# Gated DeltaNet's chunk inverses by products of nilpotent powers, and two buffers for the Mamba decays' tiles

## The chip, the cores and the metric

The kernel runs on one core of one Trainium2 chip. The metric is device time in microseconds (us), the median of three runs. Engines are named as in the profile: PE is TensorE (PEld its weight loads), DVE is VectorE, ACT is ScalarE, POOL is GpSimd, SP is SyncE, which issues the DMAs.

## The reference, cut to what matters

The model is a two-layer diffusion backbone in f32. Each layer runs three bidirectional mixers side by side on one input projection: S5, gated DeltaNet (GDN) and Mamba-2 (m2). One output projection takes all three; then comes a feed-forward part, dense SwiGLU in layer 0 and a mixture of experts in layer 1. There are 256 context and 256 latent tokens. The change is in GDN, which per chunk of tokens solves a unit lower triangular system:

```python
decay = seg_decay(gc)
lower = jnp.where(strict, jnp.einsum("bhnid,bhnjd->bhnij", kb, k) * decay, 0.0)
sol = lax.linalg.triangular_solve(jnp.eye(CHUNK) + lower, rhs,
                                  left_side=True, lower=True, unit_diagonal=True)
u_c, w_c = sol[..., :dv], sol[..., dv:]
def step(s, inp):
    v_new = u_i - w_i @ s
    s_next = s * gl_i + kd_i.T @ v_new
    o = qd_i @ s + a_i @ v_new
```

Four heads of width 128 and two directions (the second runs the tokens backwards) go through this. The kernel forms the inverse of `I + lower` itself, on blocks of 128 tokens instead of 64, and applies it by matmuls. For Mamba-2, the matrices `exp(cs_i - cs_j)` of 16 heads are the "decays".

## The kernel before, in words

The 512 tokens are four blocks t = 0..3 of 128; 0 and 1 are context, 2 and 3 latent. GDN needs one inverse X per block t, direction d and head. `inverses(gr)` (L919) makes them for two (t, d) at a time, four heads each, so every tile is 128 x 512. Four groups, grs[0] to grs[3], make the eight (t, d) of a layer; the two layers make 16.

Every group starts from an X that holds the inverses of the 16 x 16 diagonal blocks (POOL, L924). Three doublings follow, for blocks of 16, 32 and 64 (`LEVELS`). One doubling is: four transposes of X on PE (L933); four ACT evictions, one a head, that scale by beta (iv_Z, L936); four matmuls kw·Z (`mm4`, whose matmuls all have the helper's line L162); a DVE eviction that multiplies by the level's mask (iv_Q, L940); four matmuls W·X; a DVE eviction that subtracts from X (iv_X, L943). So a (t, d) makes nine trips from PE to an evicting engine and back, each needing the one before it. The matmuls of one `mm4` go to one PSUM bank, which `ps()` takes in turn from three banks ("px") in the order of the program; GDN's PE groups therefore run in program order, at most three banks apart.

The program order is: grs[0], grs[1], `steps(0)`, grs[2], `steps(1)`, in layer 0 `outs((0, 1))`, grs[3], `steps(2)`, `steps(3)`, `outs((2, 3))`. A `step` carries the state: r = v − k·S on DVE (gd_r, L963), X·r on PE, the state's update (gd_vk, gd_S), then the output A·vb (gd_vb, gd_A, gd_o). `outs` squares the outputs on ACT (gd_jk, L1013), scales them on POOL (gd_o, L1018), transposes them on PE (L1024), gates them (gd_y) and writes them to DRAM (yD).

`m2_decays` (L1060) makes the decays of four heads and one block at a time: two POOL selects, PE sums, an Exp on ACT (dq_W, L781), and a DMA to DRAM (WD, L1067). dq_W has four buffers. It makes 16 such tiles in layer 0 and 8 in layer 1. Mamba-2's later steps read them back; its tiles are m_in, m_S, m_E, m_yo, m_z and m_sq, and its last step is a norm (m_sq) and a write to yD. The output projection (tiles yr, yo; matmuls "yo,wH" and "yo,wL") reads yD back; in layer 0 in two parts, the first from S5's and GDN's rows, the second from Mamba's.

Nothing of the order around this is written out by hand. A scheduler places all instructions before the run, by the priority bands (`self.band`) that stand in Q0 and Q1, and by its own estimate of durations. Each engine then runs its list strictly in order.

Of the kernel before, what the change touches and what calls it, by code (L numbers as in the profile page):

```python
# [10 lines left out]
F32 = mybir.dt.float32  # L11
# [3 lines left out]
OP = mybir.AluOpType  # L15
# [12 lines left out]
U0, QKV0, ZG0, ZM0, XBC0 = 0, 512, 2048, 2576, 3600  # L28

CST = ["ident", "ones", "le", "ge", "gt", "lt", "blk16"]  # L30
LEVELS = [16, 32, 64]

Q0 = dict(
    pb=1.0, sc=2.5, tl=1.5, th=0.5, nb=7.5, db=1.9, ab1=0.85, ab2=3.0, sb=3.5, u=1.02, st=0.6, qkv=1.0, g0=2.0,
# [19 lines left out]
def _cst():  # L54
    i = np.arange(128)
    r, c = i[:, None], i[None, :]
    out = [r == c, np.ones((128, 128)), r <= c, r >= c, r > c, r < c, r // 16 == c // 16]
    for b in LEVELS:
        mf = ((r // b) % 2 == 1) & (c // b == r // b - 1)
        out += [mf, mf.T]  # L60
    c16 = np.arange(16)[None, :]
    out += [c16 == r % 16, c16 > r % 16, c16 < r % 16, (r // 16) % 2 == np.arange(2)[None, :]]
    return np.concatenate([np.asarray(m, np.float32) for m in out], axis=1)
# [27 lines left out]
class Net:  # L91
    def __init__(self, ctx, tc, A, out, dump=None):
        self.tc, self.nc, self.A, self.out, self.dump = tc, tc.nc, A, out, dump or {}
        nc = self.nc
        self.cpool = ctx.enter_context(tc.tile_pool(name="const", bufs=1))
        self.wstack = ctx.enter_context(ExitStack())
        self.wpool = self.wstack.enter_context(tc.tile_pool(name="wts", bufs=2, side="right"))
        self.dram = ctx.enter_context(tc.tile_pool(name="scr", bufs=1, space=DRAM))
        self.psum = ctx.enter_context(tc.tile_pool(name="psum", bufs=1, space=PSUM))
        self.psum_split(mm=(0, 1), px=(2, 3), bg=(4, 5, 6, 7), ad=(6, 7))  # L100
        c = self.cpool
        ncst = len(CST) + 2 * len(LEVELS)
        cst = c.tile([128, ncst * 128 + NC16], F32, name="cst")
        self.bands, self.ma, self.cur = {}, {}, None
        nm = len(CST) * 128
        nc.sync.dma_start(cst[:, 0:nm], A["cst"][:, 0:nm])
        with self.band(1.7):
            nc.sync.dma_start(cst[:, nm:], A["cst"][:, nm:])

        def mat(j):  # L110
            return cst[:, j * 128:(j + 1) * 128]

        for j, n in enumerate(CST):
            setattr(self, n, mat(j))
        self.mt = {}
        for j, b in enumerate(LEVELS):
            self.mt[b, 0] = mat(len(CST) + 2 * j)
            self.mt[b, 1] = mat(len(CST) + 2 * j + 1)
        c16 = cst[:, ncst * 128:]
        self.id16, self.up16, self.lo16, self.half16 = c16[:, 0:16], c16[:, 16:32], c16[:, 32:48], c16[:, 48:50]  # L120
        self.tri_r = c.tile([128, 2, 128], F32R, name="tri_r")
        nc.vector.tensor_copy(self.tri_r[:, 0, :], self.gt)
        nc.vector.tensor_copy(self.tri_r[:, 1, :], self.lt)
        self.pp = [c.tile([128, NPP], F32, name=f"pp{l}") for l in range(2)]
        for l in range(2):
            with self.band(0 if l == 0 else 1.7):
                nc.sync.dma_start(self.pp[l], A["pp"][l])
        self.epst = c.tile([128, 1], F32, name="epst")
        nc.vector.memset(self.epst, EPS)
        self.mods = [c.tile([128, 48, 2], F32, name=f"mods{l}") for l in range(2)]  # L130
        self.xT = c.tile([128, KT, T], F32, name="xT")
# [763 lines left out]
    def gdn(self, l, p, kT, qT, vD, kD, prep, nrm, bs, ks, qss, sm, szD, yD, t0, b0):  # L895
# [7 lines left out]
        def v4(ps):  # L903
            return ps.rearrange("p (h c) -> p h c", h=4)
# [13 lines left out]

        def inverses(gr):  # L919

            X = {}
            for t, d in gr:
                X[t, d] = p.tile(sh, F32, name="iv_X", bufs=Q[l]["iv"])
                nc.gpsimd.tensor_tensor(X[t, d].rearrange("p h (b c) -> p h b c", c=16),  # L924
                                        x16[d][:, 4 * t:4 * t + 4].unsqueeze(2).to_broadcast([128, 4, 8, 16]),
                                        self.blk16.rearrange("p (b c) -> p b c", c=16).unsqueeze(1).to_broadcast([128, 4, 8, 16]),
                                        op=OP.mult)
            for b in LEVELS:
                Z, W = {}, {}
                for t, d in gr:  # L930
                    pz = self.ps()
                    for h in range(4):
                        nc.tensor.transpose(pz[:, h * 128:(h + 1) * 128], X[t, d][:, h], self.ident)  # L933
                    Z[t, d] = p.tile(sh, F32, name="iv_Z", tag="iv_Z", bufs=2)
                    for h in range(4):
                        nc.scalar.activation(Z[t, d][:, h], pz[:, h * 128:(h + 1) * 128], AF.Copy, scale=bs[:, t, d, h:h + 1])  # L936
                for t, d in gr:
                    pq = mm4(lambda h: kw[t][:, h], lambda h: Z[t, d][:, h])
                    W[t, d] = p.tile(sh, F32, name="iv_Q", tag="iv_Q", bufs=2)
                    nc.vector.tensor_tensor(W[t, d], v4(pq), self.mt[b, d].unsqueeze(1).to_broadcast(sh), op=OP.mult)  # L940
                for t, d in gr:
                    px = mm4(lambda h: W[t, d][:, h], lambda h: X[t, d][:, h])
                    nc.vector.tensor_tensor(X[t, d], X[t, d], v4(px), op=OP.subtract)  # L943
            return X

        def load(t):
# [6 lines left out]
        def step(t, d, Y, last):  # L953
# [17 lines left out]
                    nc.scalar.activation(qs[:, h], pqs[:, h * 128:(h + 1) * 128], AF.Copy, scale=cs[:, h:h + 1])  # L971
            pw = mm4(lambda h: Y[:, h], lambda h: r[:, h])
            if not last:
                vk = p.tile(sh, F32, name="gd_vk", tag="iv_Q", bufs=2)
                nc.vector.tensor_tensor(vk, v4(pw), col(ks[:, t, d, :]), op=OP.mult)
                pu = mm4(lambda h: ktk[t][:, h], lambda h: vk[:, h])
                if old is not None:
                    nc.gpsimd.tensor_tensor(old, old, col(sm["tot"][:, d, t, 16:20]), op=OP.mult)
                    nc.vector.tensor_tensor(old, v4(pu), old, op=OP.add)
                else:  # L980
                    S[d] = p.tile(sh, F32, name=f"gd_S{d}", bufs=1)
                    nc.scalar.activation(S[d], v4(pu), AF.Copy)
# [24 lines left out]
        def outs(pair):  # L1007
# [12 lines left out]
            for h in (0, 2):  # L1020
                po = self.ps()
                for i in range(2):
                    for j, t in enumerate(pair):
                        nc.tensor.transpose(po[:, (2 * i + j) * 128:(2 * i + j + 1) * 128], os[t][:, h + i], self.ident)  # L1024
                y = p.tile([128, 2, 256], F32, name="gd_y", tag="iv_Z", bufs=2)
                nc.sync.dma_start(y, szD[:, h:h + 2, c])
                nc.vector.scalar_tensor_tensor(y, po.rearrange("p (h c) -> p h c", h=2), self.prm(l, "gng"), y, op0=OP.mult,
                                               op1=OP.mult)
# [31 lines left out]
    def m2_decays(self, p, sm, WD, first):  # L1060

        nc = self.nc
        for h0 in (0, 4, 8, 12):
            for t in range(first, 4):
                W = p.tile([128, 4, 128], F32, name="dq_W", bufs=4)
                self.decay_quad(p, sm, t, h0, W, "bg", 2)
                nc.sync.dma_start(WD[:, t, h0:h0 + 4], W)  # L1067

# [927 lines left out]
```

## Time and profile before

| | us |
|---|---|
| median of three runs (2482.48 to 2491.93) | 2483.15 |
| the profiled execution's own time | 2479.87 |
| its span in the trace | 2478.1 |
| PE busy in it | 2296.1 |
| DVE busy | 1868.1 |
| ACT busy | 1419.7 |
| POOL busy | 257.3 |

The profile is one execution, 3.28 us below the median. Its span leaves 1.8 us of its own time outside. The busy times overlap, so they don't add to the span. PE is busy for 93% of it, but that is an average: GDN's stretches are at 280 to 600 us (layer 0) and 1385 to 1590 us (layer 1), and there PE waits; from 1640 us on the layer-1 experts stream their weights and GDN has no part in it. A PE record's duration contains the time to pass through the array, so records in a row overlap; what a matmul costs is read from the distance of starts or from a stretch with its count.

### The profile page before, as it was taken

What the parts mean: (1) busy time and instruction counts of PE and PEld (TensorE: products, weight loads), DVE (VectorE), ACT (ScalarE), POOL (GpSimd) and SP (SyncE); (2) the same over time, 40 slices, a digit from 0 to 9 for tenths busy, and PEclk for the clock granted to TensorE, in tenths of its full rate; (3) what the DMA queues carried; (4) which work ended last, traced back from release to release, by engine and by line L of the source; (5) the groups of instructions that cost most, each with busy time, mean ns of one, the idle gap of its engine ahead of it and who ended that gap; (6) DMA issues with size and microseconds to landing.
All of it is one profiled execution on the core that took longest, in us unless ns stands there. A gap on an engine that the chain in (4) does not pass through costs nothing.

```text
span 2478.1 us, 36217 instructions
## 1 busy us (share of the span) xinstructions
PE 2296.1 (93%) x12886; PEld 1843.6 (74%) x12886; DVE 1868.1 (75%) x3138; ACT 1419.7 (57%) x2200; POOL 257.3 (10%) x332
## 2 busy tenths in 40 slices
PE   7999887898999999998998799889999999999998
PEld 4878675666767777886887677778887888888876
DVE  8887995576577773436679867678888888888887
ACT  4765475343335343235764844357777777677765
POOL 0011553212000000000021522100000000000000
PEclk9999998997999999998999899989999999999999
DMA  7443336994455755323444474478999999999994
GB/s 254 134 125 121 112 122 215 268 277 146 122 204 176 255 179 185 94 89 101 149 135 130 157 209 123 133 290 316 332 335 362 349 338 337 356 342 341 354 344 167
DMA packets 222378, 543.86 MB, mean 219 GB/s; under 512 B 25584, under 2 KB 105456, under 8 KB 186096
## 3 DMA queue, kind: packets, MB, share of 16 engines
q1 hardware_dynamic: 222192, 541.49, 63.7%
q8 instruction: 103, 1.69, 0.3%
q14 instruction: 83, 0.68, 0.1%
HBM read 487.87 MB, written 53.54 MB: 218 GB/s over the span
## 4 chain that ended last, share of the span: by engine, by line
PE 65%; DVE 6%; DMA 5%; ACT 4%; issue 3%; POOL 0%; SPq 0%; ACTq 0%; DVEq 0%; POOLq 0%
PE bank L162 62%; DMA ada<-in_ada_w_dram 1%; ACT mwH L1673 1%; DVE mwL L1674 1%; DVE wL L322 1%; PE bank L1761 1%; DMA wr<-in_w_in_dram 1%; DVE s5B L612 0%; DMA s5X<-XD 0%; DVE s5t L609 0%; DVE cv_acc L800 0%; DMA vD<-gd_tok 0%; PE bank L933 0%; DMA s5V<-VD 0%; DMA yr<-yD 0%
## 5 line engine op out<-in xcount | busy, mean ns | idle before, releaser
L1674 DVE TENSOR_TENSOR mwL<-mwr,mwH 128x2048 fp32r<-128x2048 f32 (+1 forms) x272 | 605.1, 2226 | 96.5 <-PE bank L162 60.3
L1673 ACT ACTIVATE mwH<-mwr 128x2048 fp32r<-128x2048 f32 (+1 forms) x272 | 508.2, 1869 | 201.6 <-PE bank L162 168.8
L321 ACT ACTIVATE wH<-wr 128x512 fp32r<-128x512 f32 (+2 forms) x388 | 232.8, 605 | 389.6 <-PE bank L162 241.2
L322 DVE TENSOR_TENSOR wL<-wr,wH 128x512 fp32r<-128x512 f32 (+2 forms) x388 | 267.0, 690 | 209.5 <-ACT wH L321 204.7
L162 PE MATMUL bank<-mwL,xeH 128*128 128x512 f32 (+1 forms) x768 | 292.7, 381 | 9.3 <-DVE mwL L1674 9.3
L162 PE MATMUL bank<-mwH,xeL 128*128 128x512 f32 (+1 forms) x768 | 288.1, 375 | 0.0
L162 PE MATMUL bank<-mwH,xeH 128*128 128x512 f32 (+1 forms) x768 | 284.7, 376 | 2.5 <-ACT mwH L1673 2.5
L162 PE MATMUL bank<-hH,wH 128*128 128x512 f32 (+2 forms) x656 | 245.8, 383 | 32.0 <-ACT cv_acc L798 18.6
L162 PE MATMUL bank<-hH,wL 128*128 128x512 f32 (+2 forms) x656 | 245.6, 376 | 8.7 <-DVE wL L322 8.5
L162 PE MATMUL bank<-hL,wH 128*128 128x512 f32 (+2 forms) x656 | 246.6, 376 | 1.1 <-DVE hL L300 1.1
L162 PEld LDWEIGHTS bank<-mwL,xeH 128*128 128x128 f32 x768 | 144.3, 188 | 37.7 <-DVE mwL L1674 11.7
L162 PEld LDWEIGHTS bank<-hH,wH 128*128 128x128 f32 (+1 forms) x656 | 124.0, 190 | 61.7 <-ACT cv_acc L798 20.7
L162 PEld LDWEIGHTS bank<-mwH,xeH 128*128 128x128 f32 x768 | 144.1, 188 | 32.3 <-ACT mwH L1673 3.3
L162 PEld LDWEIGHTS bank<-mwH,xeL 128*128 128x128 f32 x768 | 144.3, 188 | 26.3
L800 DVE SCALAR_TENSOR_TENSOR cv_acc<-cv_raw,pp,cv_acc 128x512 f32<-128x512 f32 (+1 forms) x192 | 152.8, 811 | 7.5 <-ACT cv_acc L796 5.8
L162 PEld LDWEIGHTS bank<-hH,wL 128*128 128x128 f32 (+1 forms) x656 | 124.4, 190 | 33.7 <-DVE wL L322 10.7
L162 PE MATMUL bank<-yo,wH 128*128 128x512 f32 (+1 forms) x512 | 133.2, 351 | 11.5 <-ACT yo L1387 7.7
L162 PEld LDWEIGHTS bank<-hL,wH 128*128 128x128 f32 (+1 forms) x656 | 124.7, 190 | 25.3 <-DVE hL L300 2.9
L162 PE MATMUL bank<-fhH,wH 128*128 128x512 f32 x352 | 137.6, 394 | 2.7 <-ACT fhH L299 1.8
L162 PE MATMUL bank<-mwL,eaH 128*128 128x512 f32 x352 | 139.2, 395 | 0.0
L162 PE MATMUL bank<-mwH,eaL 128*128 128x512 f32 x352 | 138.6, 394 | 0.0
L162 PE MATMUL bank<-fhL,wH 128*128 128x512 f32 x352 | 137.9, 392 | 0.0
(449 smaller groups left out, 4531.2 us busy)
## 6 DMA issues: line engine op xcount, KB each, us to landing
mwr<-in_moe_gu_dram SPq DMA_DIRECT2D x176, 1024.0 KB, 5.7
mwr<-in_moe_dn_dram SPq DMA_DIRECT2D x80, 1024.0 KB, 6.0
wr<-in_w_in_dram SPq DMA_DIRECT2D x160, 256.0 KB, 2.9
ada<-in_ada_w_dram SPq DMA_DIRECT2D x24, 1024.0 KB, 7.1
wr<-in_w_out_dram SPq DMA_DIRECT2D x64, 256.0 KB, 2.7
ada<-in_ada_w_dram SPq DMA_DIRECT2D x32, 512.0 KB, 6.0
wr<-in_ffn_w_gate_dram SPq DMA_DIRECT2D x44, 256.0 KB, 2.7
wr<-in_ffn_w_up_dram SPq DMA_DIRECT2D x44, 256.0 KB, 2.8
```

Source lines behind the costliest of these rows:

```text
L162: return self.nc.tensor.matmul(*a, **k)
L321: nc.scalar.activation(wH, w, AF.Copy)
L322: nc.vector.tensor_tensor(wL, w, wH.bitcast(F32), op=OP.subtract)
L800: nc.vector.scalar_tensor_tensor(acc, raw[:, :, j:j + 256], w[:, j:j + 1], acc, op0=OP.mult, op1=OP.add)
L1673: nc.scalar.activation(wH, w, AF.Copy)
L1674: nc.vector.tensor_tensor(wL, w, wH.bitcast(F32), op=OP.subtract)
L1761: nc.tensor.transpose(pt[:, j * 128:(j + 1) * 128], a[:, j * 128:(j + 1) * 128], self.ident)
```

## The change

The new `inverses` transposes X0 once and then uses a closed form. With X0 the block diagonal part's inverse and G the strictly block-triangular remainder in X0's frame, eight blocks of 16 make G⁸ = 0, so the inverse is (I − G)(I + G²)(I + G⁴)X0, read from the right side as the code builds it. F is G's mirror image, needed because PE wants the left factor transposed: G² = mm(F, G). Per (t, d): four transposes and four ACT evictions (before: twelve and twelve); masks on DVE for G and F; G² evicted by ACT (iv_G2); X −= G·X and X += G²·X on DVE; T = G²·X evicted by ACT (iv_T); X += G²·T on DVE. That is eight PSUM banks a (t, d) instead of nine, and six dependent trips from PE to an evicting engine and back instead of nine.

In numbers over both layers: PE transposes 192 → 64, PE matmuls of 128 x 128 in the inverses 384 → 448; DVE evictions of 128 x 512 96 → 80; ACT evictions of 128 x 128 192 → 64, and 32 new ones of 128 x 512. The six level masks become two masks. iv_Z and iv_Q (with the tiles that share their tags: gd_y, gd_vk) have three buffers instead of two, dq_W two instead of four. All priorities stay.

```diff
-LEVELS = [16, 32, 64]
-    for b in LEVELS:
-        mf = ((r // b) % 2 == 1) & (c // b == r // b - 1)
-        out += [mf, mf.T]
+    out += [c // 16 > r // 16, c // 16 < r // 16]
...
-            for b in LEVELS:
-                Z, W = {}, {}
-                for t, d in gr:
-                    pz = self.ps()
-                    for h in range(4):
-                        nc.tensor.transpose(pz[:, h * 128:(h + 1) * 128], X[t, d][:, h], self.ident)
-                    Z[t, d] = p.tile(sh, F32, name="iv_Z", tag="iv_Z", bufs=2)
-                    for h in range(4):
-                        nc.scalar.activation(Z[t, d][:, h], pz[:, h * 128:(h + 1) * 128], AF.Copy, scale=bs[:, t, d, h:h + 1])
-                for t, d in gr:
-                    pq = mm4(lambda h: kw[t][:, h], lambda h: Z[t, d][:, h])
-                    W[t, d] = p.tile(sh, F32, name="iv_Q", tag="iv_Q", bufs=2)
-                    nc.vector.tensor_tensor(W[t, d], v4(pq), self.mt[b, d].unsqueeze(1).to_broadcast(sh), op=OP.mult)
-                for t, d in gr:
-                    px = mm4(lambda h: W[t, d][:, h], lambda h: X[t, d][:, h])
-                    nc.vector.tensor_tensor(X[t, d], X[t, d], v4(px), op=OP.subtract)
+            for t, d in gr:
+                pz = self.ps()
+                for h in range(4):
+                    nc.tensor.transpose(pz[:, h * 128:(h + 1) * 128], X[t, d][:, h], self.ident)
+                Z[t, d] = p.tile(sh, F32, name="iv_Z", tag="iv_Z", bufs=3)
+                for h in range(4):
+                    nc.scalar.activation(Z[t, d][:, h], pz[:, h * 128:(h + 1) * 128], AF.Copy, scale=bs[:, t, d, h:h + 1])
+            for t, d in gr:
+                pg = mm4(lambda h: kw[t][:, h], lambda h: Z[t, d][:, h])
+                G[t, d] = p.tile(sh, F32, name="iv_Q", tag="iv_Q", bufs=3)
+                nc.vector.tensor_tensor(G[t, d], v4(pg), self.off[1 - d].unsqueeze(1).to_broadcast(sh), op=OP.mult)
+                pf = mm4(lambda h: Z[t, d][:, h], lambda h: kw[t][:, h])
+                F[t, d] = p.tile(sh, F32, name="iv_F", tag="iv_Z", bufs=3)
+                nc.vector.tensor_tensor(F[t, d], v4(pf), self.off[d].unsqueeze(1).to_broadcast(sh), op=OP.mult)
+            for t, d in gr:
+                p2 = mm4(lambda h: F[t, d][:, h], lambda h: G[t, d][:, h])
+                G2[t, d] = p.tile(sh, F32, name="iv_G2", tag="iv_Q", bufs=3)
+                nc.scalar.activation(G2[t, d], v4(p2), AF.Copy)
+                px = mm4(lambda h: G[t, d][:, h], lambda h: X[t, d][:, h])
+                nc.vector.tensor_tensor(X[t, d], X[t, d], v4(px), op=OP.subtract)
+            for t, d in gr:
+                px = mm4(lambda h: G2[t, d][:, h], lambda h: X[t, d][:, h])
+                nc.vector.tensor_tensor(X[t, d], X[t, d], v4(px), op=OP.add)
+            for t, d in gr:
+                px = mm4(lambda h: G2[t, d][:, h], lambda h: X[t, d][:, h])
+                tt = p.tile(sh, F32, name="iv_T", tag="iv_Z", bufs=3)
+                nc.scalar.activation(tt, v4(px), AF.Copy)
+                Z[t, d] = tt
+            for t, d in gr:
+                px = mm4(lambda h: G2[t, d][:, h], lambda h: Z[t, d][:, h])
+                nc.vector.tensor_tensor(X[t, d], X[t, d], v4(px), op=OP.add)
...
-                W = p.tile([128, 4, 128], F32, name="dq_W", bufs=4)
+                W = p.tile([128, 4, 128], F32, name="dq_W", bufs=2)
```

The scheduler places everything anew, so the instructions' order differs from the start of the program on. Three places matter below.

The first place is on PE, the end of GDN in layer 0. Before, from the last X·r (gd_r, iv_X) over the last A·vb (gd_vb) to the transposes of `outs((2, 3))` (L1024):

```order
L162 MATMUL bank_4179<-gd_r,iv_X 128x128 x4
L162 MATMUL bank_6368<-m_S_6280,m_in 128x512
L162 MATMUL bank_4188<-gd_vb,gd_A 128x128 x4
L162 MATMUL bank_6351<-m_E,m_xt 64x128 x8
L162 MATMUL bank_6351<-cst,m_yo 128x128 x4
L162 MATMUL bank_6372<-m_in 128x128
L1102 MATMUL bank_6420<-cst,m_in 128x128 x4
L1024 MATMUL bank_4223<-cst,gd_o 128x128
```

The changed kernel's rows from just ahead of the same A·vb on (s5g is S5's gate, 512 columns a matmul; L1112 is Mamba's transposes):

```order
L156 MATMUL bank_5721<-s5gH,wH 128x512
L156 MATMUL bank_5746<-s5gH,wH 128x512
L156 MATMUL bank_4084<-gd_vb,gd_A 128x128 x4
L156 MATMUL bank_5721<-s5gL,wH 128x512
L156 MATMUL bank_5721<-s5gH,wL 128x512
L156 MATMUL bank_5746<-s5gL,wH 128x512
L156 MATMUL bank_5746<-s5gH,wL 128x512
L156 MATMUL bank_6123<-m_E,m_xt 64x128 x4
L1112 MATMUL bank_6161<-cst,m_in 128x128 x4
L156 MATMUL bank_6123<-m_E,m_xt 64x128 x4
L156 MATMUL bank_6123<-cst,m_yo 128x128 x4
L156 MATMUL bank_5771<-s5gH,wH 128x512
```

From the last X·r to the first transpose of the outputs there were six rows of other or GDN work; now there are 57, with 48 matmuls of S5's gate among them.

The second place is on PE, the end of Mamba-2 in layer 0: its last norm sum (m_sq) among the output projection's matmuls (yo). Before:

```order
L162 MATMUL bank_6905<-yo,wH 128x512 x2
L162 MATMUL bank_6905<-yo,wL 128x512
L162 MATMUL bank_6905<-yo,wH 128x512 x2
L162 MATMUL bank_6905<-yo,wL 128x512
L162 MATMUL bank_6594<-m_sq,cst 128x256 x4
L162 MATMUL bank_6905<-yo,wH 128x512 x2
L162 MATMUL bank_7001<-yo,wH 128x512 x2
```

And with the change:

```order
L156 MATMUL bank_6936<-yo,wL 128x512
L156 MATMUL bank_6413<-m_E,m_xt 64x128 x4
L156 MATMUL bank_6413<-cst,m_yo 128x128 x4
L156 MATMUL bank_6439<-m_in 128x128
L156 MATMUL bank_6434<-m_S_6189,m_in 128x512
L156 MATMUL bank_6467<-m_E,m_xt 64x128 x8
L156 MATMUL bank_6467<-cst,m_yo 128x128 x4
L156 MATMUL bank_6490<-m_sq,cst 128x256 x4
L156 MATMUL bank_6858<-yo,wH 128x512
```

Between the last m_yo row and the m_sq row stood 33 matmuls of the output projection; now none stands there. Ahead of the m_sq row stood 195 of them, now 228.

The third place is on ACT in layer 0, where the decays' Exp (dq_W) meets S5's copies (s5X) and the inverses' evictions. Before, all 16 dq_W stand ahead of the bulk of s5X:

```order
L624 ACTIVATE s5X<-s5B 64x8x32
L781 ACT_TABLE_LOAD
L781 ACTIVATE dq_W<-bank_4415 128x512
L781 ACTIVATE dq_W<-bank_4427 128x512
L936 ACTIVATE iv_Z<-bank_3451,gd_bs 128x128 x4
L936 ACTIVATE iv_Z<-bank_3461,gd_bs 128x128 x4
L623 ACTIVATE s5X<-s5B 64x512
```

With the change, the last three dq_W stand among them, and so does an iv_T of grs[1]:

```order
L619 ACTIVATE s5X<-s5B 64x8x32
L949 ACTIVATE iv_T<-bank_3472 128x512
L795 ACT_TABLE_LOAD
L795 ACTIVATE cvo<-cv_acc 128x512
L775 ACT_TABLE_LOAD
L775 ACTIVATE dq_W<-bank_4299 128x512
L617 ACTIVATE s5X<-s5B 64x512
```

The iv_T stands behind eleven s5X copies, and the last dq_W 14 rows behind the one shown here.

In layer 1, S5's gate has 48 matmuls of 256 columns. Before, all stood ahead of the last row of the inverses; now all stand between that row and the last X·r, the last of them five rows ahead of the output projection's first.

## Rows read from the trace of the kernel before

**Rows 1.** The page: the chain that ended last, shares of the span by engine

```profile
PE 65%; DVE 6%; DMA 5%; ACT 4%; issue 3%; POOL 0%; SPq 0%; ACTq 0%; DVEq 0%; POOLq 0%
```

**Rows 2.** Windows: length, busy of PE, PEld, DVE, ACT, POOL (records), granted clock, DMA share, GB/s

```profile
280.00:380.00 100.00, 77.04 (x374) 60.55 (x373) 100.00 (x135) 59.87 (x103) 53.79 (x51) 0.95 0.36 117
400.00:420.00 20.00, 13.52 (x115) 10.53 (x113) 6.28 (x10) 19.73 (x32) 1.28 (x1) 0.91 0.71 230
570.00:610.00 40.00, 28.22 (x132) 20.25 (x131) 27.09 (x63) 14.39 (x45) 11.17 (x9) 0.66 0.46 146
580.00:600.00 20.00, 13.28 (x69) 10.08 (x68) 12.82 (x34) 6.96 (x27) 5.49 (x4) 0.50 0.45 145
1555.00:1590.00 35.00, 25.44 (x176) 22.98 (x174) 20.39 (x48) 9.97 (x37) 8.98 (x10) 0.85 0.24 74
```

**Rows 3.** The chain in order of time, layer 0: start, duration, what

```profile
579.13 0.78 DVE m_E L1163 x3
...
591.28 2.10 POOL gd_o L1018 x2
...
603.79 64.31 PE bank L162 x290
...
668.96 3.19 DMA yD<-m_z
672.17 4.16 DMA yr<-yD
...
678.72 21.37 PE bank L162 x85
```

**Rows 4.** PE's timeline: start, duration, instruction; records in a row overlap

```profile
1546.46 0.60 PE L933 MATMUL bank<-cst,iv_X 128*128 128x128 f32 x4
1546.82 0.36 PE L162 MATMUL bank<-s5gH,wL 128*128 128x256 f32 x1
1547.02 0.28 PE L162 MATMUL bank<-s5gH,wH 128*128 128x256 f32 x1
1547.14 0.28 PE L162 MATMUL bank<-s5gL,wH 128*128 128x256 f32 x1
...
1551.93 1.05 PE L162 MATMUL bank<-iv_Z,gd_kw 128*128 128x128 f32 x8
1552.82 1.06 PE L162 MATMUL bank<-iv_X,iv_Q 128*128 128x128 f32 x8
```

**Rows 5.** One tile, iv_X: count, duration ns min/median/max, first and last start, forms

```profile
L943 DVE TENSOR_TENSOR iv_X<-iv_X,bank x48: 673/680/690, 325.5 to 1557.1; 128x512 f32<-128x512 f32 x48
```

**Rows 6.** The same view of iv_Z, with ACT's idle time ahead of it (us, times)

```profile
L936 ACT ACTIVATE iv_Z<-bank,gd_bs x192: 350/372/433, 293.7 to 1551.4; 128x128 f32<-128x128 f32 x192
...
  PE bank L933: 35.0, 12
```

**Rows 7.** The same view of dq_W, with the landing time of its DMAs

```profile
L781 ACT ACTIVATE dq_W<-bank x24: 597/598/640, 293.3 to 1435.2; 128x512 f32<-128x512 f32 x24
L1067 SPq DMA_DIRECT2D WD<-dq_W x24: 319/326/600, 296.8 to 1435.8; - x24
...
DMA to landing us min/median/max: 2.0/2.1/6.2
```

**Rows 8.** ACT's timeline, layer 0

```profile
394.07 0.60 ACT L781 ACTIVATE dq_W<-bank 128x512 f32<-128x512 f32 x1
396.53 0.60 ACT L781 ACTIVATE dq_W<-bank 128x512 f32<-128x512 f32 x1 [1.87 <-issue]
...
421.11 0.60 ACT L982 ACTIVATE gd_S<-bank 128x512 f32<-128x512 f32 x1
```

**Rows 9.** The timeline of Mamba's last norm in layer 0

```profile
653.40 1.16 PE L162 MATMUL bank<-cst,m_yo 128*128 128x128 f32 x8
...
657.13 1.06 ACT L1189 ACTIVATE m_sq<-m_z 128x1024 f32<-128x1024 f32 x1 [5.25 <-POOL m_z L1187]
...
663.67 1.03 PE L162 MATMUL bank<-m_sq,cst 128*128 128x256 f32 x4
```

More of the change, by code (lines that the diff above doesn't have):

```diff
@@ L101, in __init__ @@
         c = self.cpool
-        ncst = len(CST) + 2 * len(LEVELS)
+        ncst = len(CST) + 2
         cst = c.tile([128, ncst * 128 + NC16], F32, name="cst")
@@ L114, in __init__ @@
             setattr(self, n, mat(j))
[L115 to L118, printed above, removed]
+        self.off = [mat(len(CST)), mat(len(CST) + 1)]
         c16 = cst[:, ncst * 128:]
@@ L919, in inverses @@
         def inverses(gr):
-            X = {}
+            X, Z, F, G, G2 = {}, {}, {}, {}, {}
             for t, d in gr:
@@ L973, in step @@
             if not last:
-                vk = p.tile(sh, F32, name="gd_vk", tag="iv_Q", bufs=2)
+                vk = p.tile(sh, F32, name="gd_vk", tag="iv_Q", bufs=3)
                 nc.vector.tensor_tensor(vk, v4(pw), col(ks[:, t, d, :]), op=OP.mult)
@@ L1024, in outs @@
                         nc.tensor.transpose(po[:, (2 * i + j) * 128:(2 * i + j + 1) * 128], os[t][:, h + i], self.ident)
-                y = p.tile([128, 2, 256], F32, name="gd_y", tag="iv_Z", bufs=2)
+                y = p.tile([128, 2, 256], F32, name="gd_y", tag="iv_Z", bufs=3)
                 nc.sync.dma_start(y, szD[:, h:h + 2, c])
```

## The prediction

> **What bounds the kernel now.** I began with the chain that ended last [rows 1]. PE is 65% of it, so PE's work and PE's waits decide, and an evicting engine matters only where PE waits for it. Next I took the windows [rows 2], to find where PE waits while GDN runs. There are four such places.
>
> First, 280 to 380 us (layer 0's first inverses): DVE is busy 100.00 of 100 us, PE 77.04. DVE bounds this stretch. Second, 400 to 420 us: ACT is busy 19.73 of 20, mostly with S5's copies. Third, 570 to 610 us (the end of GDN in layer 0): PE idles 40 − 28.22 = 11.8 us, and the granted clock is 0.66 on average; at 580 to 600 it is 0.50, which is the 1.2 GHz level. Work of 28.22 us at 0.66 loses up to 28.22 × 0.34 = 9.6 us more. Fourth, 1555 to 1590 us (the end of GDN in layer 1): 35 − 25.44 = 9.6 us idle.
>
> Then the chain in order of time [rows 3]: at the third place it goes through Mamba's m_E as well as GDN's gd_o on POOL, so two chains end there together. After 603.79 it is 64.31 us of PE without a gap, then Mamba's last write to DRAM (3.19), its read back (4.16), and the matmuls from 678.72 on. Mamba's last norm, not GDN, ends layer 0's mixers.
>
> **The change part by part.** The sum is made against the profiled execution's 2479.87 us; the median is 3.28 higher, which is added at the end.
>
> PE's own work. Four transposes take 0.36 us from their start to the next row's [rows 4], so 0.09 each; 128 fewer give −11.5. Four matmuls of 128 x 128 take 0.89 us from start to start [rows 4], so 0.223 each; 64 more give +14.3. PE's sum is **+2.8 us**: the closed form does not unload the bounding engine.
>
> DVE: 16 evictions of 0.68 us fewer [rows 5], −10.9 us in all. ACT: 128 of 0.37 us fewer [rows 6], −47.4 as records, and 32 of 0.60 us more (the nearest row is the copy of the same shape out of PSUM for dq_W [rows 7]), +19.1. ACT waited 35.0 us for the transposes in 12 waits [rows 6]; two of three such rounds go. None of this is on the path as a sum; it counts through the shorter chain of six round trips instead of nine.
>
> Here a rule of the Trainium skill speaks against the change. On ACT a 128 x 512 copy took 0.598 us and on DVE the eviction of that shape took 0.680 [rows 5, 7]. The page "ScalarE: Activation LUTs", section "Rules for kernel authors", says to put adds and multiplies on VectorE, not on ScalarE, and budgets about 0.3 us an ACTIVATE and 0.83 ns an element, which would be an estimated 0.73 us for 512 elements. By that page ACT's 32 new evictions would cost 23 us instead of 19; the trace has the shorter time.
>
> Layer 0, start. In the DVE-bound stretch four (t, d) lose one eviction each, 4 × 0.68 = −2.7 us; but PE's chain reaches into that stretch earlier, and the order puts 18 inverse evictions ahead of its end where 16 stood, +1.4. Behind it, an iv_T stands behind eleven S5 copies on ACT, and the state gd_S, which started at 421.11 right after the last copy [rows 8], is still behind all of them. So `steps(0)` starts as late as before. I take **0**, between −2.7 and +5; the upper end comes from dq_W. With two buffers the third Exp waits until the first tile has landed. The first DMA was issued 3.5 us after its Exp began, and landing took 2.1 [rows 7]: 5.6 us. Two tiles at the closest pace are 2 × 2.46 = 4.9 us apart [rows 8]; 16 × 0.7 = 11 us of ACT at worst, of which I let half reach PE.
>
> Layer 0, end of GDN. In the new order 48 gate matmuls of S5 stand between the last X·r and the transposes of the outputs. They are worth 48 × 0.222 = 10.7 us (64.31 us for 290 matmuls [rows 3]), and this is work that PE otherwise does elsewhere. GDN's chain is shorter, so it doesn't need that work beside its last inverses, and of the 11.8 us idle 10.7 can go. Of the 9.6 us of low clock I count 3.8, as POOL's 2.10 us and the transfers stay in the chain. **−14.5**, between −5.3 (half the idle, none of the clock, since Mamba's m_E waits there too) and −21.4 (everything).
>
> Layer 0, end of Mamba-2. Before, 33 output-projection matmuls stood between the last m_yo row and the last m_sq row, and covered m_in, m_z and the square: PE was done with m_yo at 654.56, the square at 658.19, and PE came to m_sq only at 663.67 [rows 9]. Now none stands there, and 33 more stand ahead. The wait of 658.19 − 654.56 = 3.6 us opens, and the 33 × 0.222 = 7.3 us are no longer there to cover the write and the read behind it (668.96 to 678.72 [rows 3]). **+10.9**, from +3.6 (only the wait) to +14.5 (the Mamba steps one row group earlier uncovered likewise, 7.3 + 2 × 3.6).
>
> Layer 1. 48 gate matmuls at 0.12 us [rows 4], 5.6 us, now stand between the last inverse and the last X·r, where PE idled 9.6 us [rows 2]: −5.6. But S5's rows come first in the output projection, the last gate matmul is only some 3.8 us of PE work ahead of it (my count along the order at these durations), and a round trip through DRAM took 3.19 + 4.16 = 7.35 us in layer 0 [rows 3]: +3.5. **−2**, between −5.6 and +3.5.
>
> Sum: 2.8 + 0 − 14.5 + 10.9 − 2 = −2.8 us, to 2477.1 for a run like the profiled one and **2480.3 beside the median**.
>
> **The rivals.** A is this sum: GDN's end gets shorter, and Mamba's end gives most of it back.
>
> B, *GDN was the bound.* All idle time and low clock at 570 to 610 goes, Mamba's end costs only its own wait, and layer 1 gains its 5.6: 2.8 − 21.4 + 3.6 − 5.6 = −20.6, **2462.5**. For it speaks that the clock there was 0.50 for 20 us; against it that the chain passed through m_E in the same stretch. The page "TensorE: Matmul & The Clock Gate" of the Trainium skill, section "Why this matters for your kernels", tells authors to avoid idle gaps between bursts of matmuls since the clock falls after them; the half clock after PE's waits agrees, and by it closing the waits gives both back.
>
> C, *slower: Mamba's last norm is the bound.* PE runs its list in order, so a wait at m_sq holds back the output projection behind it. If Mamba's chain isn't earlier, it is uncovered at +14.5, GDN's end gives only −5.3, and layer 1 shows S5's round trip without the gain: 2.8 − 5.3 + 14.5 + 3.5 = +15.5, **2498.7**. It decides where the wait ahead of m_sq and the transfers behind it exceed what GDN's end gives back. For it speaks that the chain ends in m_z, yD, yr [rows 3]; against it that Mamba's rows sit behind GDN's in the third place too and come earlier if that shortens.
>
> D, *nothing moves but work.* The round trips removed were covered by other PE work anyway, and the scheduler's new order is as good as the old: +2.8, **2486**. For it: outside the four places PE waits little.
>
> **How the numbers follow.** Chances: A 0.41, D 0.10, B 0.29, C 0.20. A and D lie within 0.5% of the median (2470.7 to 2495.6), about what a measurement of this kernel can tell from no change; I move 0.02 of A below and keep C's lower part above. That gives faster 0.31, same 0.49, slower 0.20. A's own range is 2470 to 2494, about half of the way from its sum to B's and C's ends on either side (2480.3 − 9 and + 9) and a little more for what the sum doesn't hold. The range that should hold 8 in 10 goes from B's centre to short of C's: **2462 to 2497**. The predicted time is A's, 2480.
>
> **What would show it.** In the profile after: PE's total busy time up by about 3 us at full clock, and DVE's down by some 11. At layer 0's end of GDN, the clock stays at 1.00 and idle falls from 11.8 to a few us, with s5g rows in it; if idle stays and m_E releases PE, C's view of that place is right. At layer 0's end of Mamba, PE waits some 4 us at m_sq and 7 us more for yr; if out_proj's first part still fills that time, B holds. DVE at 100% through the first inverses, and gd_S right behind the last S5 copy, show the start unchanged; an Exp waiting for WD's landing shows the buffers' price. In layer 1, the first output-projection matmul waiting for yr with S5's rows confirms the last term. The prediction is wrong altogether if the new order shifts other waits, for instance in the loads that share SP's queue, by more than these terms: the sum holds only the four places.

## The result, and the profile after

The changed kernel takes 2501.49 us (median of six runs, 2496.28 to 2505.16) beside 2483.18 for the kernel before (now of six runs, too): 1.0068 times as long, 95% interval 1.0056 to 1.0081. I forecast 2480 and a range of 2462 to 2497; that was wrong. The time lies just past rival C (2498.7), which I had given 2 chances in 10.

The profiled execution has a span of 2498.7 us (2500.42 in all), 20.6 above the span before. The page by engine (busy us, share of the span, instructions):

```profile
PE 2302.8 (92%) x12886; PEld 1850.5 (74%) x12886; DVE 1848.6 (74%) x3122; ACT 1403.1 (56%) x2104; POOL 253.0 (10%) x332
```

DVE and ACT are busy for 20 and 17 us less, less in both as the counts said, though not by those sizes, and the whole is slower all the same. The windows that answer to [rows 2], with one more at 680 us and layer 1's moved by 20 us (length, busy of PE, PEld, DVE, ACT, POOL with records, granted clock, DMA share, GB/s):

```profile
280.00:380.00 100.00, 83.14 (x432) 67.21 (x432) 99.97 (x137) 55.17 (x88) 49.90 (x49) 0.97 0.31 104
400.00:420.00 20.00, 9.47 (x64) 7.87 (x62) 3.36 (x5) 19.70 (x27) 3.77 (x4) 0.71 0.37 135
570.00:610.00 40.00, 30.94 (x123) 19.44 (x122) 24.43 (x54) 20.76 (x45) 9.11 (x8) 0.83 0.61 202
680.00:700.00 20.00, 6.34 (x14) 4.46 (x15) 5.83 (x10) 3.65 (x4) 1.28 (x3) 0.53 0.23 79
1575.00:1610.00 35.00, 28.58 (x191) 25.00 (x190) 23.27 (x56) 15.81 (x43) 8.09 (x8) 0.85 0.42 126
```

The stretch at 570 to 610 us is better: PE 30.94 busy instead of 28.22, the clock 0.83 instead of 0.66. The one at 400 to 420 is worse, 9.47 instead of 13.52. And 680 to 700 is new: 6.34 of 20 us, at about half clock. What happens there is in the timeline around Mamba's last norm of layer 0 (start, duration, engine, line, instruction; in brackets the idle time before it and what ended it), which answers to [rows 9]:

```profile
674.00 1.12 PE L156 MATMUL bank<-m_E,m_xt 128*64 128x128 f32 x8 [4.09 <-DVE m_E L1174]
675.43 1.12 PE L156 MATMUL bank<-m_E,m_xt 128*64 128x128 f32 x8 [0.30 <-DVE m_E L1174]
676.48 1.80 PE L156 MATMUL bank<-cst,m_yo 128*128 128x128 f32 x8
...
680.82 1.06 ACT L1199 ACTIVATE m_sq<-m_z 128x1024 f32<-128x1024 f32 x1 [7.42 <-POOL m_z L1197]
681.92 3.78 PE L156 MATMUL bank<-m_sq,cst 128*128 128x256 f32 x8 [3.65 <-ACT m_sq L1199]
...
689.97 0.38 SPq L1209 DMA_DIRECT2D yD<-m_z  x1
692.89 0.80 SPq L1396 DMA_DIRECT2D yr<-yD  x2
...
697.44 2.07 PE L156 MATMUL bank<-yo,wH 128*128 128x512 f32 x4 [11.73 <-ACT yo L1397]
```

Before, PE came to that norm at 662.80 (the row in [rows 9], at 663.67, is only the second half of the norm's matmuls) with its square long done (658.19), and had other output-projection matmuls to do through most of the write and read back [rows 3]. Now it waits 4.09 us for m_E, 3.65 for the square, and 11.73 for the rest of the norm, the transfers and the rounding of yo behind them. The norm is at 681.92, so 19.1 us later. The feed-forward part's first matmul comes at 745.34; before it came at 725.42. These 19.9 us pass through to the end: layer 1's output projection starts 20.7 us later, the span is 20.6 longer.

### The profile page after: what moved, and what is told of

Its sections match the earlier page's. It is cut to its first block, busy times and chain, and to the rows that moved or that the text cites. A ratio compares the mean times of both kernels' runs of the same rounds, so it can differ in the third digit from the quotient of the medians.

```text
span 2498.7 us, 36086 instructions
## 1 busy us (share of the span) xinstructions
PE 2302.8 (92%) x12886; PEld 1850.5 (74%) x12886; DVE 1848.6 (74%) x3122; ACT 1403.1 (56%) x2104; POOL 253.0 (10%) x332
## 4 chain that ended last, share of the span: by engine, by line
PE 72%; DVE 11%; DMA 7%; ACT 5%; issue 3%; SPq 1%; POOL 1%; ACTq 0%; DVEq 0%; POOLq 0%
PE bank L156 70%; DVE cv_acc L794 2%; DVE wL L316 2%; DVE s5B L606 1%; DVE s5t L603 1%; DVE mwL L1684 1%; DMA s5D<-KD 1%; DMA ada<-in_ada_w_dram 1%; ACT mwH L1683 1%; PE bank L1771 1%; DMA wr<-in_w_in_dram 1%; PE bank L506 1%; DMA s5V<-VD 1%; ACT wH L315 1%; DMA yr<-yD 1%
## 5 line engine op out<-in xcount | busy, mean ns | idle before, releaser
L156 PE MATMUL bank<-hH,wH 128*128 128x512 f32 (+2 forms) x656 | 245.6, 382 | 28.0 <-ACT cv_acc L792 15.7
```

The costliest lines, as they stand in the source:

```text
L156: return self.nc.tensor.matmul(*a, **k)
```

## Experiments

The twelve were timed in three rounds (E1 to E4, E5 to E8, E9 to E12), each in turn with the kernel before on the same chip; its medians there were 2485.85, 2484.24 and 2484.04, and each ratio below is against its own round. My theory at the start (1): the whole loss is in layer 0, where Mamba's last norm comes late in PE's list, and whatever pushes it back costs. Rival 1: PE's early waits behind S5's copies on ACT. Rival 2: the two dq_W buffers. A third rival came up on the way.

### The parts of the change

E1, the old algebra with the new buffers:

```diff
-                    Z[t, d] = p.tile(sh, F32, name="iv_Z", tag="iv_Z", bufs=2)
+                    Z[t, d] = p.tile(sh, F32, name="iv_Z", tag="iv_Z", bufs=3)
-                    W[t, d] = p.tile(sh, F32, name="iv_Q", tag="iv_Q", bufs=2)
+                    W[t, d] = p.tile(sh, F32, name="iv_Q", tag="iv_Q", bufs=3)
-                W = p.tile([128, 4, 128], F32, name="dq_W", bufs=4)
+                W = p.tile([128, 4, 128], F32, name="dq_W", bufs=2)
```

(gd_vk and gd_y share those tags and are changed alike.)

> The kernel before with its three doublings, but with the change's buffers: iv_Z and iv_Q three each, dq_W two. It tells the buffers from the new algebra. In its PE order Mamba's third norm (m_sq) of layer 0 already stands later than before (by some 15 us of PE work) and the last one some 8 us later. Theory 1 (the last Mamba norm, pushed back in PE's list, ends layer 0; whatever pushes it costs): +5 to +12 us, about 2488 to 2495, all of it in layer 0. Rival 1 (the new algebra's PE waits behind S5's copies on ACT at 400 to 420 us cost the time): this kernel has no iv_T, so within 3 us of the kernel before, 2480 to 2486. Rival 2 (two dq_W buffers cost it): the full +18, about 2500.

Measured: 2491.9, ratio 1.0025 (1.0014 to 1.0037), so 6 us slower, as theory 1 had it. Its timeline has the same two waits as the changed kernel (m_sq, and yo behind the transfers) with no new algebra in it:

```profile
669.76 3.78 PE L162 MATMUL bank<-m_sq,cst 128*128 128x256 f32 x8 [4.02 <-ACT m_sq L1189]
...
685.46 2.07 PE L162 MATMUL bank<-yo,wH 128*128 128x512 f32 x4 [11.92 <-ACT yo L1387]
```

E2 and E3, the new algebra in one layer only; both keep the new buffers:

```diff
+            for b in LEVELS if l == OLD else ():
...
+            if l == OLD:
+                return X
```

> The changed kernel with the three doublings put back in layer 1 alone (the six old masks are loaded as well). Its PE order in layer 0 is that of the changed kernel. If layer 0 holds the whole loss, as the two traces say (the feed-forward part starts 19.9 us later, the end comes 20.6 us later), 2497 to 2503. If the new algebra in layer 1 gives or costs something by itself that the later start hides, off from the changed kernel's 2501 by that.

> The other half: the three doublings in layer 0, the new algebra in layer 1, all with the change's buffers. Theory 1: as the kernel with old algebra and new buffers within 3 us, since layer 1's mixers took the same time in both traces. If layer 1's algebra were worth its shorter chain, 4 to 6 us below that kernel.

Measured: E2 2500.24 (1.006, 1.0044 to 1.0077) and E3 2491.09 (1.0024, 1.0013 to 1.0034). E2 is the changed kernel's time, E3 is E1's. So the new algebra costs some 9 us in layer 0 and neither gives nor takes anything measurable in layer 1. The waits for m_sq and yo alone don't make these 9 us, since E1 has both. Up to the feed-forward part's first matmul PE idles 104.9 us in the changed kernel and 97.7 in E1, and is busy 640.4 and 635.7; E1 has no wait for m_E ahead of its last norm.

E4, four dq_W buffers beside the new algebra:

```diff
-                W = p.tile([128, 4, 128], F32, name="dq_W", bufs=2)
+                W = p.tile([128, 4, 128], F32, name="dq_W", bufs=4)
```

> The changed kernel with four dq_W buffers again, one part of the change undone. Rival 2 (an Exp waits for a DMA's landing): most of the +18 comes back, 2483 to 2487. Theory 1: what decides is where Mamba's last norm stands in layer 0's PE list. In this kernel's order it stands some 60 us of PE work earlier, and S5's gate 28 us later than in the changed kernel, right ahead of the output projection. So the Mamba wait goes (-10 to -20 against the changed kernel) but S5's gate and its trip through DRAM may take its place: 2480 to 2500, with the first output-projection matmul later than the changed kernel's 593 us.

Measured: 2545.98, ratio 1.0235. Both theories missed, by 46 us and more. The view of dq_W's instructions (count, ns min/median/max, first and last start) shows why:

```profile
L775 ACT ACTIVATE dq_W<-bank x24: 577/597/602, 487.1 to 1497.2; 128x512 f32<-128x512 f32 x24
```

The first Exp runs at 487.1 us; in the changed kernel it runs at 293.6. GDN's last output transposes stand at 483.76 in this trace, so the decays begin only once GDN is through. I take it that the decays' tiles with four buffers don't fit beside GDN's with three and get their memory after it; that is argued from the order of the two, not shown. What is shown is that in this kernel the two-buffer dq_W is what lets the decays, and with them all behind them, start early.

E11, two dq_W buffers in the kernel before and nothing else (`bufs=4` to `bufs=2`):

> The kernel before with two dq_W buffers and nothing else. Every engine's list is the same, row for row, so only the waits of an Exp for a DMA's landing can differ. Theory 1: those are hidden, within 3 us of the kernel before, 2481 to 2487. The bound I gave such waits was up to 5 us on PE: 2488.

Measured: 2485.13, ratio 1.0009 (0.9991 to 1.0027). In the old order the two buffers by themselves cost nothing that can be measured. In the changed kernel's trace no Exp waits for a landing, and PE waits 0.2 us in all for a dq_W. Rival 2 falls.

### Early waits, or Mamba's place

E5, three priorities of layer 0, nothing else changed against the changed kernel:

```diff
-    gd=1.0, gl=1.1, g1=2.0, xb=2.0, m2=4.0, yo0=4.5, yo1=1.0, yo2=1.67, yo3=5.0, parts=0, w=0.8, gdl=1.0, gdo=1.0,
-    m2o=3.9, m2g=4.0, qk=1.0, qq=1.0, qv=1.0, sm=1.0, gi1=1.12, gl3=1.12, sg=3.2, qo=(1, 0, 2), gx=0, wr=3, wh=4,
+    gd=1.0, gl=1.1, g1=2.0, xb=2.0, m2=3.0, yo0=4.5, yo1=1.0, yo2=1.67, yo3=5.0, parts=0, w=0.8, gdl=1.0, gdo=1.0,
+    m2o=2.9, m2g=3.0, qk=1.0, qq=1.0, qv=1.0, sm=1.0, gi1=1.12, gl3=1.12, sg=3.2, qo=(1, 0, 2), gx=0, wr=3, wh=4,
```

> The changed kernel with three numbers of layer 0's priorities changed and nothing else: Mamba-2's steps, outputs and norms (m2 4.0, m2o 3.9, m2g 4.0) to 3.0, 2.9, 3.0, so that they go ahead of S5's gate (3.2). In PE's list Mamba's third and last norms of layer 0 then stand at 502 and 542 us of PE work (changed kernel 537 and 565, kernel before 501 and 556). Theory 1 (the +9.5 of the algebra beyond the buffers' +6 is Mamba's rows pushed back in the list): Mamba's last m_sq matmul some 15 us earlier than 682, and 2481 to 2491 in all. Rival 1 (PE's waits for iv_T and gd_S behind S5's copies at 400 to 420 us): these are still there, so 2497 to 2503.

Measured: 2485.55, ratio 1.0005 (0.9993 to 1.0018). The loss is gone with the algebra and the buffers in place. The norm comes 24 us earlier than in the changed kernel, at full clock, with no wait at it:

```profile
657.62 1.89 PE L156 MATMUL bank<-m_sq,cst 128*128 128x256 f32 x8
```

E6, G² and T evicted by DVE, so that no iv_T stands behind S5's copies:

```diff
-                nc.scalar.activation(G2[t, d], v4(p2), AF.Copy)
+                nc.vector.tensor_copy(G2[t, d], v4(p2))
-                nc.scalar.activation(tt, v4(px), AF.Copy)
+                nc.vector.tensor_copy(tt, v4(px))
```

> The changed kernel with the 32 evictions of G^2 and T as DVE copies instead of ACT copies. DVE does 32 more of about 0.6 us, ACT 32 fewer; nothing stands behind S5's copies any more. Rival 1: PE's waits at 400 to 420 us for iv_T (6.5 us) go, 2491 to 2496. Theory 1: Mamba's last norm stands at 565 us of PE work as in the changed kernel and its third at 552 instead of 537, so no gain: 2498 to 2506.

Measured: 2504.98, ratio 1.0076 (1.0052 to 1.0099). Theory 1's number. PE's wait for iv_T is gone, but its wait for gd_S behind the same copies is longer (6.51 us, 5.19 in the changed kernel), and at the end the same two waits stand (the one for yo is 11.81 us):

```profile
421.68 2.07 PE L156 MATMUL bank<-gd_vk,gd_ktk 128*128 128x128 f32 x8 [6.51 <-ACT gd_S L992]
...
683.81 3.38 PE L156 MATMUL bank<-m_sq,cst 128*128 128x256 f32 x8 [3.64 <-ACT m_sq L1199]
```

E6 removed only one of rival 1's two waits, so it says nothing of the second. E5 does: PE still waits 4.09 us for iv_T and 4.88 for gd_S there, idles 9.6 us at 400 to 440 (13.8 in the changed kernel), and yet the loss is gone. E10 below has the two waits at 5.95 and 5.22, nearly as long as the changed kernel, and no loss either. Rival 1 falls as the cause of the loss.

E8, E5 and E6 together:

> Both: new algebra, Mamba's steps ahead of S5's gate, and G^2 and T evicted by DVE. Mamba's last norm stands at 557 us of PE work, against 542 with the priorities alone. Theory 1: some 5 to 10 us slower than the priorities alone, about 2490 to 2497. Rival 1: 5 to 7 us faster than the priorities alone.

Measured: 2487.68, ratio 1.0015 (1.0003 to 1.0026). Against E5's 2485.55 that is 2 us more, within the two intervals. Theory 1 wanted 5 to 10 us more, rival 1 5 to 7 less; by the medians both missed.

E9 and E10, E5's priorities one after the other: only the states (`m2=3.0`), then the states and the outputs (`m2=3.0`, `m2o=2.9`). The third rival is that Mamba's late start at 440 to 520 us costs the time, not its late end.

> The changed kernel with one priority of layer 0 changed: Mamba's states (m2 4.0 to 3.0), its outputs and norms (m2o, m2g) left. Mamba's first work then comes as early as with all three priorities (first norm at 418 us of PE work, 420 there, 439 in the changed kernel), but the last norm stands where it does in the changed kernel, at 565 (542 with all three). It tells an early start of Mamba from an early end. Theory 1 (the last norm's place ends layer 0): 2496 to 2503, as the changed kernel. Rival 3 (Mamba's late start at 440 to 520 us is what costs): 2483 to 2490.

> The same with two priorities changed (m2 3.0, m2o 2.9, norms left at 4.0): the last norm stands at 552 us of PE work, between the 542 of all three and the 565 of the changed kernel. Theory 1: between the two, 2489 to 2496. Rival 3: 2483 to 2490.

Measured: E9 2499.21, ratio 1.0073 (1.0054 to 1.0091), and E10 2479.79, ratio 0.9989 (0.9977 to 1.0001). In E9 Mamba's first norm is at 488.50, ahead of the kernel before (500.81), but the last one is at 671.13 and PE waits there as in the changed kernel (11.89 us for yo behind it). Rival 3 falls:

```profile
671.13 2.73 PE L156 MATMUL bank<-m_sq,cst 128*128 128x256 f32 x8 [4.03 <-ACT m_sq L1199]
```

E10 was expected between E5 and the changed kernel and has the lowest median of all; both expectations missed. So the norm's place in the list alone doesn't set the time. In E10's windows PE is busy 48.59 of 60 us at 560 to 620 and 58.58 of 60 at 620 to 680; in E5's, with Mamba's norms ahead too, 42.69 and 59.93:

```profile
560.00:620.00 60.00, 48.59 (x273) 34.32 (x269) 39.70 (x89) 31.41 (x70) 9.83 (x9) 0.91 0.69 219
620.00:680.00 60.00, 58.58 (x275) 45.53 (x274) 40.42 (x83) 21.48 (x40) 5.75 (x6) 1.00 0.46 143
```

```profile
560.00:620.00 60.00, 42.69 (x239) 28.92 (x237) 44.85 (x97) 30.64 (x73) 11.44 (x10) 0.88 0.63 202
620.00:680.00 60.00, 59.93 (x271) 47.01 (x272) 36.33 (x70) 20.21 (x33) 4.46 (x5) 0.95 0.45 145
```

The first pair is E10's, the second E5's. In E5 the output projection starts at 616.64, in E10 at 611.03. My reading is that the projection must start early enough to fill PE, and leave enough matmuls to cover Mamba's last transfers. It is not shown: the two intervals overlap, and of E10's 6.6 us at the feed-forward part 2.8 are left at layer 1's first input-projection matmul (1143.52, in E5 1146.27), while at layer 1's output projection 9.6 us lie between the two (1572.40, 1582.01). Most of the difference arises in layer 1, whose priorities are the same.

E7 and E12, the same three priorities in the kernel before, and in E1:

> The kernel before with the same three priorities (3.0, 2.9, 3.0). It tells whether the priorities are worth something by themselves. Mamba's last norm stands at 544 us of PE work instead of 556, S5's gate 16 us later. If the old kernel's order was already balanced: within 5 us of it, 2481 to 2491, since out_proj's first rows come later. If Mamba's last norm alone ends the layer here too, 2473 to 2480.

> The old three doublings with the change's buffers and the three Mamba priorities, to be set beside the new algebra under the same buffers and priorities (2485.55). Mamba's last norm stands at 545 us of PE work there, 542 with the new algebra. If the algebra itself is worth what I counted for GDN's shorter end, 5 to 15 us slower, 2490 to 2500; if the algebra is worth nothing once Mamba's place is the same, 2483 to 2488.

Measured: E7 2488.61, ratio 1.0019 (1.0008 to 1.003); E12 2483.62, ratio 1.0009 (0.999 to 1.0028). E12 beside E5 (2485.55) is old algebra against new, with equal buffers and equal priorities: no difference in the whole time that can be told. Equal priorities are not equal places, though. In the profiled executions E12's last norm is 9.8 us earlier than E5's and its feed-forward part starts 15.6 us earlier; of that 8.6 us are left in the spans (2475.7 and 2484.3) and 1.9 in the medians. So in these two executions the old algebra has the shorter layer 0.

E7 has a surprise. Its feed-forward part starts at 711.00, 14.4 us earlier than in the kernel before, and the whole is not faster. Part of the gain goes in the feed-forward part: PE waits for the ada weights' DMAs between 760 and 1000 us, for which it doesn't wait in the kernel before (PE's waits: us in total, times, longest):

```profile
PE bank L162 <- DMA ada<-in_ada_w_dram: 7.7, 3, 4.1
```

Of the 14.4 us 7.4 are left at layer 1's first input-projection matmul (1140.40, before 1147.83) and 1.3 at layer 1's output projection (1579.58, before 1580.88). E12 loses its lead likewise, without those waits: 11.5 us at the feed-forward part, 9.6 at the input projection (1138.22), 5.1 at the output projection (1575.81). Why the later parts take it back is not shown.

### All of it side by side

From the timelines of the profiled executions (us): the start of Mamba's last norm on PE in layer 0, PE's wait for the second part of the output projection, the feed-forward part's first matmul, and the execution's own time; then the median of all runs, and the ratio to the kernel before in the same round.

| kernel | last norm | wait for yo | feed-forward | this execution | median | ratio |
|---|---|---|---|---|---|---|
| before | 662.80 | 3.75 | 725.42 | 2479.87 | 2483.18 | 1 |
| E7 old, Mamba first | 643.94 | none | 711.00 | 2480.78 | 2488.61 | 1.0019 |
| E12 old, new buffers, Mamba first | 647.83 | none | 713.92 | 2477.36 | 2483.62 | 1.0009 |
| E8 new, Mamba first, DVE | 659.22 | 3.62 | 721.93 | 2483.12 | 2487.68 | 1.0015 |
| E11 old, two dq_W | 659.37 | 4.21 | 722.48 | 2481.7 | 2485.13 | 1.0009 |
| E10 new, states and outputs first | 660.72 | 1.13 | 722.92 | 2479.06 | 2479.79 | 0.9989 |
| E5 new, Mamba first | 657.62 | none | 729.55 | 2486.03 | 2485.55 | 1.0005 |
| E3 new in layer 1 only | 668.37 | 11.99 | 732.75 | 2489.64 | 2491.09 | 1.0024 |
| E1 old, new buffers | 669.76 | 11.92 | 733.46 | 2491.55 | 2491.9 | 1.0025 |
| E9 new, states first | 671.13 | 11.89 | 735.45 | 2493.31 | 2499.21 | 1.0073 |
| E2 new in layer 0 only | 677.15 | 12.15 | 741.44 | 2494.46 | 2500.24 | 1.006 |
| changed kernel | 681.92 | 11.73 | 745.34 | 2500.42 | 2501.49 | 1.0068 |
| E6 new, evictions on DVE | 683.81 | 11.81 | 746.84 | 2508.3 | 2504.98 | 1.0076 |
| E4 new, four dq_W | 654.02 | none | 776.48 | 2545.66 | 2545.98 | 1.0235 |

The six that are slower than the kernel before by 5 to 21 us are the six that wait some 12 us there; E4, whose decays start late, is slow without that wait. Among the others the feed-forward part's start goes from 711.00 to 729.55 and doesn't order the medians. So a late end of layer 0 was passed on to the whole time, and an early one was not, or not measurably. The medians don't follow the column to the microsecond either: single executions differ from their medians by up to 8 us (E7).

## Why the prediction was wrong, step by step

**PE's own work** was forecast at +2.8 us. PE's busy time rose by 6.7, which holds work at low clock too. Right in sign; small either way.

**DVE, ACT.** −10.9 and −28 us forecast; −19.5 and −16.6 measured over the whole page. The inverses' evictions alone make −10.7 of DVE's (65.4 to 54.7), as forecast; most of the rest is Mamba's m_E (37.0 to 29.1 on one line), which is not part of the change. On ACT they make −16.4 (53.8 to 37.4). There the term was too large because the short evictions overlap as records: eight take 2.18 us, 0.27 each, and were priced at 0.37. The row called a copy in the sum is an Exp; the change's own copies (iv_G2, iv_T) took a median of 0.597 us, so its price held, and 0.688 on DVE (iv_T in E6). The rule that the prediction takes from the Trainium skill is on adds and multiplies; these evictions are plain copies. That they are off the path agrees with E6, where 32 of them change engines and no difference can be told (2504.98 beside 2501.49).

**Layer 0, start.** Forecast 0, between −2.7 and +5. GDN's first step starts 10.5 us earlier (gd_vp at 406.88, before 417.36), not "as late as before". The state gd_S, from which I argued, is in its old place (420.74, before 421.11), and PE waits for iv_T (6.50) and gd_S (5.19) behind S5's copies. PE's idle time from 280 to 440 us is 38.2, before 35.2, and the clock at 400 to 420 is 0.71, before 0.91. The wait that I named is there; that it would leave the sum alone was too kind by some 3 us of idle and the low clock. E10 has both waits without a loss, so they aren't what makes the change slower.

**Layer 0, end of GDN.** Forecast −14.5. GDN's last transposes come 15.3 us earlier (578.12, before 593.42) and the output projection starts 14.9 earlier (593.38, before 608.27). The number is met and the step failed all the same, for the time doesn't come out of PE's idle time. The windows from 280 us to the output projection's start and from there to the feed-forward part's first matmul, before and then after:

```profile
280.00:608.27 328.27, 272.44 (x1811) 206.03 (x1809) 240.29 (x416) 166.82 (x365) 111.51 (x99) 0.92 0.64 195
608.27:725.42 117.15, 107.27 (x472) 80.26 (x471) 73.38 (x163) 39.00 (x69) 5.76 (x6) 0.97 0.45 143
```

```profile
280.00:593.38 313.38, 259.14 (x1739) 195.81 (x1738) 214.58 (x374) 157.54 (x308) 105.70 (x98) 0.93 0.63 198
593.38:745.34 151.96, 124.03 (x543) 91.72 (x543) 85.73 (x193) 45.13 (x83) 9.10 (x8) 0.87 0.37 124
```

Up to the projection's start PE idles 54.2 us, before 55.8: only 1.6 less. The rest is work that moved: 72 records fewer stand ahead of the start, 13.3 us of busy time, and they are all Mamba's (32 for m_E, 16 for m_yo, the others for m_in, m_sq and m_bt); they stand behind it now. So the projection started earlier because Mamba's rows made room, and that 14.9 agrees with 14.5 is luck. With the new algebra and Mamba's outputs ahead again it starts later than before, at 611.03 in E10 and 616.64 in E5, with GDN's last transposes at 593.73 and 585.57. I counted as a gain of the layer what was a gain of a chain that doesn't end it. The idle time at 570 to 610 fell only from 11.8 to 9.1 us, and 4.65 of the 9.1 are now PE's wait for the projection's own first rows.

**Layer 0, end of Mamba-2.** Forecast +10.9, with the upper end at +14.5. This is the term that was mis-sized. The wait at m_sq was forecast at 3.6 us and is 3.65. The part for the write and read back was put at 7.3; PE waits 11.73 there, before 3.75, so 8.0 more. The m_E wait ahead of it, which I had put only in the upper end, is 4.09. Together 3.65 + 8.0 + 4.09 = 15.7 us, above my upper end, and PE runs 680 to 700 at a granted clock of 0.53, which the term left out altogether. In the second pair of windows PE idles 27.9 us, before 9.9, so 18.0 more. From the kernel's start to the feed-forward part's first matmul it is 104.9 beside 87.9: 17.0 of the 19.9 us that layer 0 takes longer are PE's waits, nearly all of them at Mamba's end. I had read the same falling clock out of the kernel before [rows 2] and priced it only as a gain of closing gaps, not as a cost of opening one.

**Layer 1.** Forecast −2; from the feed-forward part on the traces say +0.7, and E2 and E3 say nothing measurable. The idle time at GDN's end fell from 9.6 to 6.4 us, less than the 5.6 forecast. The wait for S5's rows, +3.5 in the sum, didn't come: PE waits 2.86 us at the output projection's start, before 3.98.

**The choice between the cases.** I wrote that Mamba's norm, not GDN, ends layer 0's mixers, and then still added GDN's gain in full to the sum. If the last chain is Mamba's, a shorter GDN can only help through Mamba's rows coming earlier, and the order showed them later: 33 more output-projection matmuls ahead of the norm, none left to cover it. Rival C said this and gave 2498.7. E5, E9 and E10 show that it was the right rival: move Mamba's outputs ahead in the list and the loss goes, move only its states and it stays. That C's number is so near is in part luck, since its +3.5 in layer 1 didn't come and its 0 at layer 0's start was too low. D's reading, that the algebra is worth nothing by itself, agrees with E5 beside E12 in the whole time; Mamba's place was not the same in these two.

**The change's parts.** I counted the third iv buffers at nothing and didn't put them in the sum. Beside two dq_W buffers they cost 6 us without any new algebra (E1), and the waits are again those at Mamba's norm. The wait for dq_W's landing, up to 5 us in my bound, is nothing that can be measured (E11), though what stands in the place of the two buffers is not the old kernel but E4's 2546.

What stays open, besides why an early end of layer 0 isn't passed on, is why the scheduler, with the priorities unchanged, puts Mamba's outputs later when GDN gets shorter or has more buffers. E5, E9 and E10 show that raising Mamba's outputs (m2o) along with its states past S5's gate undoes it, and its states alone don't; its own estimates, by which it decides, stand in no trace. No version measured beats the kernel before clearly: E10's interval, 0.9977 to 1.0001, reaches 1.

## What to carry to other kernels

Before a gain on one chain is added to a sum, name the chain that ends the stage; if it is another one, the gain is only what that other chain gets of it. When priorities were set for one set of durations and a step gets shorter, look in the new order for who fills the freed time: here it was the output projection, which was then missing as cover at the last transfer. Buffers alone can move a scheduler's order much as an algorithm does (6 us here, beside some 9), so time them apart.

## What the hardware showed

The eight m_sq records took 1.89 us in E5, where PE came to them from full work and the granted clock was 1.00. In the changed kernel, where PE had idled for 6.0 of the 10 us before, they took 3.78 at a granted clock of 0.50: exactly double, the 1.2 GHz level instead of 2.4. The section "Why this matters for your kernels" of "TensorE: Matmul & The Clock Gate" in the Trainium skill says to avoid idle gaps between bursts of matmuls; the trace agrees, and the waits in front of this short step cost their own length here and then doubled the step's time. The DMA of a dq_W tile took a median of 3.0 us to land in the changed kernel, 2.1 before [rows 7], which I had not expected. Two buffers don't do it alone: in the old order the median was 2.3 (E1) and 2.4 us (E11). In E5, with a median of 3.0, one Exp waited 5.4 us for a landing, without a loss in the whole time.
